# Group A's probabilities are turned in 32x32 blocks on VectorE instead of on TensorE

## The chip, the core and the metric

The kernel runs on one core of a Trainium2 chip. A core has a matrix engine (TensorE, PE in the profile, with its weight loader PEld), three engines for element-wise work (VectorE or DVE, ScalarE or ACT, GpSimd or POOL), a queue engine that mostly issues transfers (SyncE, SP), an on-chip memory of 128 partitions (SBUF) and a small accumulator memory of eight banks that TensorE writes (PSUM). The metric is the time of one execution in device microseconds. The kernel before took 2522.41 us (median of three runs, 2521.24 to 2526.48).

## What is computed

A trunk of two layers over 1024 tokens of width 1024, in float32. In each layer a normed input is projected and shared out to four groups of attention heads, whose outputs are joined, projected and added to the input; then comes an MLP with a squared ReLU.

- Group A: four heads with latent queries, keys and values; dense attention over all 1024 keys, score depth 96, value width 64.
- Group B: four differential heads; each needs two dense softmaxes, value width 64.
- Group C: banded attention over 128 tokens either side. Group D: neighbourhood attention on a 64-wide grid.

For group A the reference is, for each block of 128 queries:

```python
s = jnp.einsum('bqhd,bkhd->bhqk', qi, k, preferred_element_type=jnp.float32) * scale
p = jax.nn.softmax(s, axis=-1)
return jnp.einsum('bhqk,bkhd->bqhd', p.astype(v.dtype), v)
```

The outputs of A, C and D are each divided by their root mean square over 256 columns (the mix norm) before the output projection.

## The kernel before

Activations lie with features on partitions and tokens along the free dimension. Numbers that need float32 accuracy are split into a high and a low part, and a product takes three TensorE passes (`passes`): high x high, high x low, low x high. A split needs an activation on ScalarE and a subtraction on VectorE or GpSimd.

**Order of the work.** The program is not issued in the order in which it is written. Each engine call is recorded as a step in a plan (`Plan.add`) with a price (`Plan.price`); each stage has a window of due times (`SPAN`, in units of a layer of 1250), and a step's rank is its place in that window by TensorE's prices. `Plan.order` then imitates the engines and the transfer queues: whichever engine is free next takes, of the steps that can start, the one with the lowest rank. Steps inside `together()` are issued without a break. The resulting order is fixed in the program for each engine, so stages overlap as ranks and prices have it.

**Places.** A tile needs a place before a step can use it: 40 places of 1024 floats per partition ("pair"), 19 of 512 ("half"), some small ones, and the 8 PSUM banks. Tiles with one tag also have a cap. A place is free again when the tile's last reader is done.

**Stages of a layer** (`attention`): the projections of B, the latent inputs, D and C; `latent_up`, which makes A's queries, keys and values from the latent parts and stores them to DRAM; the attention of B, D, C and A; for each group the mix norm; the output projection in two parts. The first part, "o1", takes for four output tiles ("front") what needs groups B and D only, and for four others ("back") what needs B, D and C; each back tile then holds a PSUM bank until the second part, "o2", which needs group A's mix (mix tiles 6 and 7). Then comes the MLP, with products of 512 columns that share sums in the manner of Strassen (`mlp_up`, `mlp_down`).

**Dense attention before** (`dense`, used by A and B). For each tile of 128 queries, `softmax` makes two banks of 512 scores with three matmuls each, VectorE reduces each bank to a row minimum while it writes the negated scores to a tile p, and ScalarE takes the exponential of p with its row sum. The probabilities have queries on partitions, while the value product needs keys there. So TensorE transposes p, 128x128 at a time:

```python
nc.tensor.transpose(t[:, k * 256 + i * P:k * 256 + (i + 1) * P],
                    p[:, (j * 2 + k) * P:(j * 2 + k + 1) * P], self.ident)
```

Four transposes fill a bank, which is copied to SBUF (tag pt) by VectorE and ScalarE in turn (`transposed`). For each pair of query tiles eight float32 matmuls follow, each with 128 keys by 64 value columns as weights and 256 columns of turned probabilities moving:

```python
nc.tensor.matmul(out[k * 64:(k + 1) * 64], v[:, j * 2 + k], pts[j][:, k * 256:k * 256 + 256],
                 start=n == 0, stop=n == 3)
```

Even key tiles land in partitions 0 to 63 of the bank and odd ones in 64 to 127: two column tiles of the array. `pv_out` adds the two halves (a ScalarE copy, tag pvt, and a VectorE add into y). A float32 matmul leaves two records of TensorE in the profile. At a head's end `denominators` sends the reciprocals of the row sums through DRAM and back as a tile that is spread over partitions (rz), and y is multiplied by it.

A layer's group A so has 4 heads x 8 query tiles x 6 score matmuls, 4 x 64 transposes, 4 x 16 copies and 4 x 32 product matmuls.

**The way from group A to the second part of the projection.** y, the reciprocals' trip through DRAM, the product, squares, a column sum on TensorE (`rstd_cols`), a transpose of its result (`rows_of`), a second trip through DRAM, two products, and the split to the mix tiles (`mix_group`, `mixed`).

## Time and profile before

| | before |
|---|---|
| median of three runs | 2522.41 us |
| the profiled execution | 2517.78 us |
| its span, first to last instruction | 2516.0 us |
| mean granted TensorE clock | 0.996 |
| TensorE, weight loader | 2467.4 us, 1967.1 us |
| VectorE, ScalarE, GpSimd | 1909.8, 1290.5, 379.7 us |
| bytes moved by DMA | 378.56 MB |

The profile is that of one execution. Busy time of an engine is the union of its instructions; matmuls are pipelined, so the sum of their durations is more than their busy time. A row of a group reads: line, engine, operation, output<-inputs by the program's tile names, shapes, xcount, then busy us and mean ns of one, then the idle time of the engine in front of them and what ended it. Every instruction has the same line (677), because the plan issues them all from one place; groups are told apart by tile names: "stack" is a score operand, "p" a tile of probabilities, "ident,p" a transpose of it, "pt" turned probabilities, "bank" any PSUM tile, CUSTOM_DVE_ANT_0 the reduction to a row minimum. A row of the timeline reads: start us, duration us, engine, line, operation, tiles, shapes, xcount.

### The profile page before, as it was taken

The numbers are of one execution on the slowest core, as the hardware profiler recorded it, in microseconds if no ns is written. First come the engines' busy times: TensorE is split into PE (matmuls) and PEld (weight loads), VectorE is DVE, ScalarE is ACT, GpSimd is POOL, SyncE is SP. The second block draws the span as 40 slices with busy tenths as digits, with TensorE's granted clock in tenths as the row PEclk, the third lists the DMA queues.
The fourth block names the chain that finished last, engine by engine and source line by source line (L and its number), as shares of the span: only waits on it lengthen the run. The fifth ranks groups of instructions, "written<-read, shape, count | busy, mean of one in ns | idle before, by whom it ended". The sixth has DMA issues, their size and how long they took to land.

```text
span 2516.0 us, 35396 instructions
## 1 busy us (share of the span) xinstructions
PE 2467.4 (98%) x12332; PEld 1967.1 (78%) x12332; DVE 1909.8 (76%) x3576; ACT 1290.5 (51%) x2397; POOL 379.7 (15%) x258
## 2 busy tenths in 40 slices
PE   8999999999999999999999999999999999999998
PEld 6777776778888887888877777677788888888887
DVE  7767867775877779888777677677678777898887
ACT  4545757653644445444425456666455444444454
POOL 3323224213000000000042231332140000000000
PEclk9999999999999999999999999999999999999999
DMA  5534478622244457444154344885123444665431
GB/s 180 180 112 133 122 218 234 197 80 72 78 165 159 151 202 271 147 142 139 72 182 130 119 117 135 232 255 170 46 70 117 155 155 158 231 231 158 130 105 67
DMA packets 190514, 378.56 MB, mean 150 GB/s; under 512 B 24112, under 2 KB 36352, under 8 KB 190336
## 3 DMA queue, kind: packets, MB, share of 16 engines
q1 hardware_dynamic: 175360, 350.09, 44.6%
q10 hardware_dynamic: 14976, 26.22, 2.7%
q8 instruction: 97, 1.59, 0.3%
q14 instruction: 81, 0.66, 0.1%
HBM read 260.15 MB, written 116.07 MB: 150 GB/s over the span
## 4 chain that ended last, share of the span: by engine, by line
PE 83%; DVE 8%; DMA 4%; ACT 2%; issue 2%; SPq 1%; POOL 0%; DVEq 0%; POOLq 0%; ACTq 0%
PE bank L677 83%; DVE p L677 2%; DVE part L677 1%; SPq L677 1%; ACT p L677 1%; DVE x L677 1%; DMA a<-in_w_down 1%; DVE sq L677 1%; DMA acts<-ev 1%; DVE col L677 0%; DMA latp<-lat 0%; DMA c<-in_w_down 0%; DVE xl L677 0%; DVE ev L677 0%; DVE both L677 0%
## 5 line engine op out<-in xcount | busy, mean ns | idle before, releaser
L677 PE MATMUL bank<-far,wh 128*128 128x512 f32 (+1 forms) x2848 | 870.3, 387 | 1.1 <-ACT wh L677 0.6
L677 PEld LDWEIGHTS bank<-far,wh 128*128 128x128 f32 x2848 | 532.4, 188 | 110.5 <-ACT wh L677 1.4
L677 PE MATMUL bank<-far,wl 128*128 128x512 f32 (+1 forms) x1424 | 550.3, 387 | 2.7 <-DVE wl L677 2.7
L677 ACT ACTIVATE p<-p,col 128x1024 f32<-128x1024 f32 (+2 forms) x320 | 294.6, 921 | 196.3 <-DVE col L677 194.2
L677 POOL TENSOR_TENSOR wl<-ws,wh 128x512 fp32r<-128x512 f32 (+1 forms) x138 | 191.1, 1390 | 1180.2 <-ACT wh L677 1089.8
L677 PEld LDWEIGHTS bank<-far,wl 128*128 128x128 f32 x1424 | 267.4, 188 | 57.9 <-DVE wl L677 3.4
L677 PE MATMUL bank<-stack 96*128 96x512 f32 (+2 forms) x896 | 285.0, 395 | 5.0 <-DVE col L677 2.3
L677 DVE TENSOR_TENSOR x<-bank,x 128x512 f32<-128x512 f32 (+1 forms) x276 | 187.2, 680 | 121.9 <-PE bank L677 121.0
L677 PE MATMUL bank<-ident,p 128*128 128x128 f32 x1376 | 253.6, 276 | 10.4 <-DVE part L677 4.8
L677 PE MATMUL bank<-xh,wh 128*128 128x512 f32 x608 | 250.9, 413 | 3.1 <-ACT wh L677 2.6
L677 PE MATMUL bank<-xh,wl 128*128 128x512 f32 x608 | 250.6, 413 | 1.1 <-POOL wl L677 1.1
L677 PE MATMUL bank<-xl,wh 128*128 128x512 f32 x608 | 250.6, 412 | 0.0
L677 PEld LDWEIGHTS bank<-ident,p 128*128 128x128 f32 x1376 | 171.3, 141 | 59.5 <-issue 10.7
L677 PEld LDWEIGHTS bank<-stack 96*128 96x128 f32 (+1 forms) x896 | 159.3, 189 | 43.8 <-DVE col L677 12.1
L677 ACT ACTIVATE pt<-bank 128x512 f32<-128x512 f32 (+2 forms) x256 | 137.5, 556 | 82.9 <-PE bank L677 75.2
L677 DVE TENSOR_TENSOR wl<-raw,wh 128x512 fp32r<-128x512 f32 x224 | 150.3, 690 | 34.5 <-ACT wh L677 34.0
L677 PE MATMUL bank<-pt,v 128*64 128x256 f32 (+2 forms) x1344 | 173.1, 396 | 2.2 <-ACT pt L677 2.0
L677 ACT ACTIVATE ev<-ev 128x512 f32<-128x512 f32 x128 | 80.6, 632 | 160.3 <-DVE ev L677 155.8
L677 DVE CUSTOM_DVE_ANT_0 p<-bank,zero,col 128x512 f32<-128x512 f32 x192 | 143.8, 749 | 22.2 <-PE bank L677 5.1
L677 PE MATMUL bank<-mix,wh 128*128 128x512 f32 x512 | 160.3, 393 | 0.0
L677 DVE CUSTOM_DVE_ANT_0 p<-bank,zero 128x512 f32<-128x512 f32 x192 | 131.7, 686 | 35.4 <-PE bank L677 34.1
L677 ACT ACTIVATE wh<-raw 128x512 fp32r<-128x512 f32 x224 | 135.4, 621 | 23.8 <-ACT ev L677 10.5
(158 smaller groups left out, 3904.5 us busy)
## 6 DMA issues: line engine op xcount, KB each, us to landing
act<-acts SPq DMA_DIRECT2D x224, 256.0 KB
raw<-in_w_up SPq DMA_DIRECT2D x128, 256.0 KB
acts<-ev SPq DMA_DIRECT2D x128, 256.0 KB
acts<-ev ACTq DMA_DIRECT2D x96, 256.0 KB
ws<-in_w_in SPq DMA_DIRECT2D x76, 256.0 KB
c<-in_w_down SPq DMA_DIRECT2D x64, 256.0 KB
rz<-drows SPq DMA_DIRECT2D x40, 256.0 KB
ws<-in_w_out SPq DMA_DIRECT2D x40, 256.0 KB
```

What stands on the lines that cost most here:

```text
L677: getattr(s.eng.engine, s.op)(*[real(a) for a in s.args], **{k: real(a) for k, a in s.kw.items()})
```

## The change

For group A alone `dense` is replaced by `turned`. VectorE turns each tile of probabilities in 32x32 blocks, SBUF to SBUF: two calls of 128x512 for a query tile. A block turn leaves each block in its own strip of 32 partitions, so strip a holds, for each of the 32 key blocks of 32 keys, the queries a*32 to a*32+31 of every query tile. All eight query tiles of a head are written side by side into two new wide places of 4096 floats, so that each key block has 256 columns in each strip. The value products then are matmuls of 32 keys (one strip) by 64 value columns with 256 columns moving: 16 pairs of key blocks x 2 halves x 4 strips = 128 for a head, in one unit without a break, into four PSUM banks, one a strip. They are written for the head behind, after the third query tile's turns of the next one. The values must lie in all four strips, so `vrows` loads them four times.

The two wide places ("quad") take the room of eight pairs, so 32 pairs remain. In the other stages the wide places hold the last normed operands of the input projections, the latent parts of `latent_up`, two of `mlp_up`'s operands and the operands 1, 6, 4 and 3 of `mlp_down`. The plan's price of a float32 matmul is divided by the number of tiles that fit the array (8 for the new form) instead of by two, group A's window starts at 400 instead of 405, and o1's window is 430 to 545 instead of 505 to 550. `Plan.issue` keeps the number of tiles as its mode, and A's probabilities no longer pass through tag pt.

```diff
...
@@ -397,10 +397,10 @@
             if op == "transpose":
                 return 108.0, 53.0
             if moving.dtype == F:
-                s.tiled = cols >= 128 and (out.arr.shape[0] <= 64 or s.args[1].arr.shape[0] <= 64)
-                if s.tiled:
-                    return max(4 * cols / 2.4 + 13, 224) / 2, cols / 2.4 * 2
-                return max(4 * cols / 2.4 + 13, 224), cols / 2.4 * 4
+                tiles = 128 // max(32, out.arr.shape[0]) * (128 // max(32, s.args[1].arr.shape[0]))
+                s.tiled = tiles if cols >= 128 and tiles > 1 else 0
+                tiles = max(s.tiled, 1)
+                return max(4 * cols / 2.4 + 13, 224) / tiles, cols / 2.4 * 4 / tiles
             return (max(cols / 2.4 + 14, 112) if cols >= 128 else 112), cols / 2.4
         if q == "scalar":
             d = 0.832 * n + (50 if psum else 94)
...
@@ -598,7 +598,7 @@
             if slow:
                 occ, lat = occ * 1.89, lat * 2
             self.act[k] = self.act.get(k, 0.0) + lat
-            s.done = t + occ * (2 if s.tiled else 1) + 180 * (1.5 if slow else 1)
+            s.done = t + occ * max(s.tiled, 1) + 180 * (1.5 if slow else 1)
             return t + occ
         if q in ("vector", "gpsimd"):
             wide = [v for v in s.ins if math.prod(v.arr.shape[1:]) > 1]
@@ -625,7 +625,7 @@
         if tag in self.CAPS:
             bufs = self.CAPS[tag].get(stage, bufs)
             tag += stage
-        kind = "pair" if n > 512 else "half" if n > P else "row" if n > 16 else "col"
+        kind = "quad" if n > S else "pair" if n > 512 else "half" if n > P else "row" if n > 16 else "col"
         return self.plan.cell(shape, dt, tag="%s%d" % (tag, bufs), cap=bufs, kind=kind, name=name or tag)
 
 
@@ -651,12 +651,13 @@
         self.xp, self.big, self.wp, self.cp = place(8), place(16), place(3), place(2)
         self.place = place()
 
-    PLACES = {"pair": 40, "half": 19, "row": 3, "col": 30, "bank": 8}
+    QUADS = 2
+    PLACES = {"quad": QUADS, "pair": 40 - 4 * QUADS, "half": 19, "row": 3, "col": 30, "bank": 8}
 
     def home(self, c):
         if c.kind in self.still:
             return self.still[c.kind][c.slot]
-        n = 1024 if c.kind == "pair" else 512
+        n = {"quad": 4096, "pair": 1024, "half": 512}[c.kind]
         return self.data.tile([P, n], c.dt, tag=f"{c.kind}{c.slot}", name=f"{c.name}")
 
     def fixed(self, shape, name, dt=F):
@@ -956,8 +957,15 @@
                     self.keep(saved[k], self.x[k])
                 ahead = None
             xs, acc = [None] * 8, None
+            places = []
             for k in chain(*(range(4 * c, 4 * c + 4) for c in (l, 1 - l))):
-                h, lo = self.big_tile(R, f"xh{k}"), self.big_tile(R, f"xl{k}")
+                if not places:
+                    if k % 2 == 0 and (k % 4 // 2 + 2 * (k // 4 != l)) >= 4 - self.QUADS:
+                        q = self.place.tile([P, 4, S], R, tag="quad", bufs=self.QUADS, name="xq")
+                        places = [q[:, i] for i in range(4)]
+                    else:
+                        places = [self.big_tile(R, f"xh{k}"), self.big_tile(R, f"xl{k}")]
+                h, lo = places.pop(0), places.pop(0)
                 for sl in self.halves(1 if l or k else 2):
                     self.split(h[:, sl], lo[:, sl], self.x[k][:, sl], scale=self.g1[:, l, k:k + 1])
                 xs[k] = (h, lo)
@@ -1044,11 +1052,13 @@
                 share(self.mm_ps(), m, 1, self.weights(w_out[m, 0]) + self.weights(w_out[m, 1]), range(8))
 
     SPAN = {"open": (0, 60), "b1": (62, 95), "lat": (270, 325), "pd": (95, 170), "pc": (170, 270), "b": (65, 330),
-            "d": (230, 390), "up": (335, 390), "c": (300, 405), "a": (405, 510), "mb": (345, 350), "md": (405, 410),
-            "mc": (415, 420), "ma": (515, 520), "o1": (505, 550), "o2": (550, 600), "mlp": (600, 1220)}
+            "d": (230, 390), "up": (335, 390), "c": (300, 405), "a": (400, 510), "mb": (345, 350), "md": (405, 410),
+            "mc": (415, 420), "ma": (515, 520), "o1": (430, 545), "o2": (550, 600), "mlp": (600, 1220)}
     LAYER, SOON, IDLE = 1250, 20, 12
-    BANKS = {"mm": 8, "tr": 4, "sb": 2, "pv": 2}
+    BANKS = {"mm": 8, "tr": 4, "sb": 2, "pv": 2, "pq": 4}
     EARLY, NP = 4, 6
+    AFTER = 2
+    WIDE = {6, 4, 3}
     WAVES = [(T_BQ[t], T_BK[t], T_BV[t]) for t in range(2)]
 
     def table(self, name, rb, eng):
@@ -1186,14 +1196,16 @@
 
     def latent_up(self, l, lat, rows, qa, ka, va):
         nc, d = self.nc, self.d
-        rq, rkv = self.big_tile(F, "rq"), self.big_tile(F, "rkv")
+        quads = [self.place.tile([P, 4, S], R, tag="quad", bufs=self.QUADS, name="latp") for _ in range(2)]
+        rq, rkv = (quads[1][:, i].bitcast(F) for i in (2, 3))
+        tiles = iter([quads[0][:, i] for i in range(4)] + [quads[1][:, i] for i in range(2)])
         self.spread(rq, rows[0], 0, 2)
         self.spread(rkv, rows[0], 1, 2)
         parts = []
         for i, r in ((0, P), (1, 64), (2, P)):
             p = []
             for j in range(2):
-                t = self.big_tile(R, "latp")
+                t = next(tiles)
                 for at in range(0, P, r):
                     self.load(t.bitcast(F)[at:at + r], lat[j, i, :r])
                 p.append(t)
@@ -1358,6 +1370,59 @@
             products()
         yield True
 
+    def vrows(self, src):
+
+        src = src.rearrange("(q r) k d -> r q (k d)", q=4)
+        tiles = []
+        for i in range(2):
+            v = self.place.tile([P, 2, 8, 64], F, tag="vr", bufs=4, name="v")
+            for a in range(4):
+                self.load(v[a * 32:a * 32 + 32].rearrange("p q k d -> p q (k d)"), src[:, 2 * i:2 * i + 2])
+            tiles.append(v)
+        return tiles
+
+    def turned(self, heads):
+
+
+        nc = self.nc
+        rows = [slice(a * 32, a * 32 + 32) for a in range(4)]
+
+        def products(job):
+            t, v, y, h2, done = job
+            pv = [self.bank("pq")[:, 0:256] for _ in rows]
+            with self.plan.together():
+                for n in range(16):
+                    for c in range(2):
+                        k, q = divmod(2 * n + c, 4)
+                        for r, ps in zip(rows, pv):
+                            nc.tensor.matmul(ps[c * 64:c * 64 + 64], v[q // 2][r, q % 2, k], t[n // 8][r, 2 * n + c & 15],
+                                             start=n == 0, stop=n == 15)
+            o = y[h2 * 64:h2 * 64 + 64].rearrange("p (t a j) -> p a t j", a=4, j=32)
+            for i in range(2):
+                other = self.place.tile([P, 512], F, tag="pt", bufs=self.NT, name="pvt")[0:64]
+                for j in range(2):
+                    ps, e = pv[2 * i + j], other[:, j * 256:j * 256 + 256]
+                    nc.scalar.activation(e, ps[64:128], AF.Copy)
+                    self.tt(o[:, 2 * i + j], ps[0:64].rearrange("p (t j) -> p t j", j=32),
+                            e.rearrange("p (t j) -> p t j", j=32), ALU.add)
+            done()
+
+        job = None
+        for head in heads:
+            probs, *rest = head()
+            t = [self.place.tile([P, 16, 256], F, tag="quad", bufs=self.QUADS, name="turn") for _ in range(2)]
+            for i in range(8):
+                p = probs(i)
+                for n in range(2):
+                    nc.vector.transpose(t[n][:, :, i * 32:i * 32 + 32],
+                                        p[:, n * 512:n * 512 + 512].rearrange("p (b j) -> p b j", j=32))
+                if i == self.AFTER and job:
+                    products(job)
+            job = (t, *rest)
+            yield True
+        products(job)
+        yield True
+
     def attn_b(self, l, t, qb, kb, vb, out):
         nc = self.nc
         pair = {}
@@ -1430,7 +1495,7 @@
                 tl.append(s[0:96])
             qh, kh, ql, kl = tl
             passes = [(qh, kh), (qh, kl), (ql, kh)]
-            v = self.vtile(va[h])
+            v = self.vrows(va[h])
             z = self.col("za", 8)
 
             def probs(qt):
@@ -1443,7 +1508,7 @@
 
             return probs, v, y, h2, done
 
-        yield from self.dense([lambda h=h: head(h) for h in range(4)])
+        yield from self.turned([lambda h=h: head(h) for h in range(4)])
         ys += [y for y, _ in out]
 
 
@@ -1637,6 +1702,10 @@
         t = self.place.tile([P, 2, 512], dt, tag=tag, bufs=bufs, name=tag)
         return t[:, 0], t[:, 1]
 
+    def wide(self):
+        t = self.place.tile([P, 4, 2, 512], R, tag="quad", bufs=self.QUADS, name="wide")
+        return [(t[:, k, 0], t[:, k, 1]) for k in range(4)]
+
     def rows_split(self, t, src, scale=None):
 
         self.split(t[0], t[1], src, scale)
...
@@ -1791,7 +1860,7 @@
                 for s in first:
                     s.w11 = self.weight_parts(s.c["11"], "we", 4)
                     combos(s.c)
-            places = [near(c) for c in "abc"]
+            places = [near() if i < self.QUADS else [self.twin("opc", R) for _ in range(4)] for i in range(3)]
             ops[2] = [self.rows_split(places[0][k], x(k + 4, 0), gk(k + 4)) for k in range(4)]
             for s in first:
                 p12(s)
@@ -1874,14 +1943,15 @@
                     return out
 
                 def op(o):
-                    return [self.rows_split(self.far(), t) for t in raw_op(o)]
+                    to = self.wide() if o in self.WIDE else [self.far() for _ in range(4)]
+                    return [self.rows_split(p, t) for p, t in zip(to, raw_op(o))]
 
                 M = range(4)
                 u = [self.bank("u") for _ in M]
                 with self.plan.sooner(0 if j else self.SOON):
                     a11 = [w(2 * i + e, 0, t) for i in range(2) for e, t in enumerate(self.twin("a"))]
                     t = raw_op(1)
-                b = [self.rows_split(self.far(), v) for v in t]
+                b = [self.rows_split(p, v) for p, v in zip(self.wide(), t)]
                 for m in M:
                     self.block(u[m], a11[m], b)
                     add(m, 0, u[m])
```

More of the change, by code (lines that the diff above doesn't have):

```diff
@@ L316, in add @@
         s.unit.steps.append(s)
-        s.start, s.tiled = None, False
+        s.start, s.tiled = None, 0
         before = set()
@@ L452, in order @@
         self.act, self.slow, self.window = {}, {0: True}, 0
-        self.mode = False
+        self.mode = 0
         for u in units:
@@ L1674, in mlp_up @@
         with self.banks(u=2, p=2, q=2, mm=2):
-            near = lambda tag: [self.twin("op" + tag, R) for _ in range(4)]
+            near = self.wide
             far = self.far
```

## The prediction

> **What bounds the kernel now.** I read the page's head first, then its chain, then busy time by stretch, then the stretch in which group A is computed, by groups of instructions.
>
> ```profile
> span 2516.0 us, 35396 instructions
> ...
> PE 2467.4 (98%) x12332; PEld 1967.1 (78%) x12332; DVE 1909.8 (76%) x3576; ACT 1290.5 (51%) x2397; POOL 379.7 (15%) x258
> ...
> PE 83%; DVE 8%; DMA 4%; ACT 2%; issue 2%; SPq 1%; POOL 0%; DVEq 0%; POOLq 0%; ACTq 0%
> ```
>
> TensorE is busy for 98% of the span and makes 83% of the chain that ended last: what is taken off TensorE shortens the time, as long as nothing else becomes the bound. That has to be read by stage. In layer 0, 442 to 549 is group A's attention (its first score matmul starts at 442.01), 549 to 600 mostly the first half of the output projection, 600 to 645 its second half; 1684 to 1791 is group A again in layer 1.
>
> ```profile
> core 0: us, PE busy (x) PEld busy (x) DVE busy (x) ACT busy (x) POOL busy (x), PEclk, DMA share, GB/s
> 340.00:442.00 102.00, 95.67 (x577) 70.38 (x577) 70.90 (x187) 68.00 (x176) 42.09 (x28) 0.98 0.85 243
> 442.00:549.00 107.00, 106.55 (x715) 80.56 (x714) 80.19 (x192) 72.95 (x126) 19.85 (x10) 1.00 0.50 151
> 549.00:600.00 51.00, 51.00 (x255) 40.91 (x254) 25.70 (x39) 14.61 (x29) 11.80 (x11) 1.00 0.18 50
> 600.00:645.00 45.00, 45.00 (x201) 37.24 (x200) 38.26 (x49) 29.37 (x51) 21.26 (x14) 1.00 0.27 74
> ...
> 1684.00:1791.00 107.00, 106.07 (x709) 79.74 (x707) 79.80 (x190) 72.10 (x125) 19.79 (x10) 1.00 0.51 150
> ```
>
> In group A's stretch TensorE has no hole (106.55 of 107), but VectorE stands at 80.19 already. The two layers agree, so I work out layer 0 and double it. A full 512-column matmul costs TensorE 0.224 us (201 in 45.00). The groups of the stretch 442 to 549, and rows of TensorE and of its weight loader in order of time:
>
> ```profile
> L677 PE MATMUL bank<-stack 96*128 96x512 f32 x192 | 54.1, 411 | 0.0
> L677 PE MATMUL bank<-ident,p 128*128 128x128 f32 x248 | 35.8, 275 | 0.1
> ...
> L677 PE MATMUL bank<-pt,v 128*64 128x256 f32 x228 | 27.9, 386 | 0.0
> L677 DVE CUSTOM_DVE_ANT_0 p<-bank,zero,col 128x512 f32<-128x512 f32 x32 | 24.0, 749 | 4.1 <-PE bank L677 0.6 <-DVE col L677 0.2
> L677 DVE CUSTOM_DVE_ANT_0 p<-bank,zero 128x512 f32<-128x512 f32 x32 | 22.0, 686 | 6.4 <-PE bank L677 6.3
> L677 DVE COPY pt<-bank 128x512 f32<-128x512 f32 x29 | 19.9, 686 | 10.8 <-PE bank L677 10.8
> L677 ACT ACTIVATE pt<-bank 128x512 f32<-128x512 f32 x30 | 17.6, 587 | 10.8 <-PE bank L677 10.7
> ...
> L677 DVE TENSOR_TENSOR y<-bank,pvt 64x512 f32<-64x512 f32 x7 | 4.8, 680 | 0.1
> ```
> ```profile
> 442.01 0.48 PE L677 MATMUL bank<-stack 96*128 96x512 f32 x1
> ...
> 505.01 1.95 PE L677 MATMUL bank<-pt,v 128*64 128x256 f32 x16
> ...
> 508.16 1.04 PE L677 MATMUL bank<-ident,p 128*128 128x128 f32 x8
> ```
> ```profile
> 507.93 1.03 PEld L677 LDWEIGHTS bank<-ident,p 128*128 128x128 f32 x8
> ```
>
> The reader is to see three prices. A transpose takes (1.04 - 0.275)/7 = 0.109 us from start to start. A product matmul leaves two records, and two column tiles run abreast: 16 records are 8 rounds, (1.95 - 0.386)/7 = 0.22 us a round. And VectorE's half-score copy, its negated-score reductions and its adds over 512 columns all take about 0.69.
>
> **The change part by part.** Per layer group A has 4 heads of 8 query tiles.
>
> Removed from TensorE: 4 x 64 transposes x 0.109 = 27.9 us. Removed with them: 64 copies out of PSUM, 32 on VectorE (32 x 0.686 = 22.0) and 32 on ScalarE (18.8, off the path).
>
> Added to VectorE: 16 block turns a head, 64 a layer, of 128x512. No row shows one. Bounds: 0.553 and 1.299, a copy of 384 columns and an operation that passes over 1024:
>
> ```profile
> L677 DVE COPY pt<-bank 128x384 f32<-128x384 f32 x48 | 26.5, 553 | 17.1 <-PE bank L677 16.6
> L677 DVE TENSOR_TENSOR sq<-sq 128x1024 f32<-128x1024 f32 x20 | 26.0, 1299 | 2.3 <-ACT sq L677 2.3
> L677 DVE TENSOR_TENSOR part<-bank,rb 128x256 f32<-128x256 f32 x48 | 18.1, 419 | 24.6 <-PE bank L677 24.5
> ```
>
> I take 0.686, the copy of the same shape: 43.9 a layer. The result adds become 16 of 256 columns (0.419, 6.7) instead of 8 of 512 (5.4). VectorE in the stretch: 80.2 - 22.0 + 43.9 + 1.3 = 103.4 of 107.
>
> Products: 128 matmuls of 32 rows by 64 columns a head, 256 records, instead of 64. If all eight tiles run abreast these are 32 rounds x 0.22 = 7.0 us, as now (32 rounds). No row shows row tiles side by side. Bounds: 7.0, and 256 x 0.11 = 28.2 if only the column pair overlaps. I take 7.0, because the pair shows that tiles are independent. One entry into the tiled mode a head goes instead of two; the drain is a fraction of a microsecond, nothing.
>
> The Trainium skill speaks against the full factor ("TensorE: Matmul & The Clock Gate", Part 3: Packing small matmuls): four row tiles were measured at 3.07 times, not 4. By it a head's products would take 9.1 us, by my row 7.0; the sum below would end 17 us later, at an estimated 2512, inside the forecast's own range. No run here shows it yet.
>
> So TensorE's own work for group A falls to about 107 - 28 = 79 us and VectorE's rises to 103: **VectorE becomes the bound of this stage.** The output projection's first part is moved forward (its window now starts at 430) to fill TensorE. It can't fill all: the products take four PSUM banks, the scores two, and each of the four back tiles holds a bank to the second half.
>
> A new wait: the two wide places hold one head. The next head's turns wait until the products have read them, the first place after half (3.5 us), the second after 7.0. Queued behind that on VectorE is the next head's softmax: one tile's pair of reductions is ready (0.749 + 0.686 = 1.4), then VectorE is out of scores, since TensorE is in the products. It idles about 2 us in the first half and 1.6 after three turns (3 x 0.69) in the second: 3.6 a head, 11 over three changes. VectorE's other work here (scaling, mixing; 9.5 us, what the four groups above leave of 80.2) covers some of it. I take 8.
>
> End of group A: 442 + 103.4 + 8 = 553.4, then the last head's products 7.0 and their reading 1.5: 562 (now 559.0, below). Then comes the chain of norms that nothing shortens but less waiting:
>
> ```profile
> 558.34 0.69 DVE L677 TENSOR_TENSOR y<-bank,pvt 64x512 f32<-64x512 f32 x1
> ...
> 569.12 1.23 DVE L677 TENSOR_TENSOR sq<-sq 128x1024 f32<-128x1024 f32 x1 [1.13 <-ACT sq L677]
> ...
> 575.22 1.84 PE L677 MATMUL bank<-ones,sq 128*128 128x1 f32 x16
> ...
> 578.08 0.17 DVE L677 SCALAR_TENSOR_TENSOR col<-col,col 128x8 f32<-128x8 f32 x1
> ...
> 583.18 0.27 PE L677 MATMUL bank<-ident,col 128*8 128x128 f32 x1
> ...
> 592.42 2.55 ACT L677 ACTIVATE mix<-y,par 128x512 fp32r<-128x512 f32 x4
> ...
> 644.07 0.39 PE L677 MATMUL bank<-mix,wl 128*128 128x512 f32 x1
> ```
>
> It lasts 592.4 - 559.0 = 33.4, of which 575.22 - 570.35 = 4.9 and 583.18 - 578.25 = 4.9 are waits for a TensorE that was busy with the projection. TensorE has holes now, so 9.2 of these go: 24.2. Group A's mix stands at 586.2, its first half is split 1.4 later (0.64 on ScalarE, by the row of four, 0.69 on VectorE, and the hand-over), and 192 matmuls x 0.224 = 43.0 are left: 630.6, against 644.3 now. Gain 13.7 a layer, **27.4 in all**. If TensorE's holes also take the 24 matmuls of the front tiles that need only group C, 5.4 more a layer.
>
> At nothing, with cover: values are fetched four times over, in 8 transfers of 128 KB a head instead of one of 256 KB, into a stretch where DMA is at 0.50; SP's extra issues are short, there are places for two heads' values, and these are needed only 20 us after a head's first score. The latent parts and the MLP's operands move into the wide places: same instructions, same operand depth, TensorE full there. Forty paired places become 32 beside the wide ones: bound, from nothing to the 6.3 us in which TensorE already waits in 340 to 442 (95.67 of 102) doubled; I take nothing.
>
> The profiled execution took 2517.78 us (1.8 around its span), 4.6 below the median of 2522.41, a gap of its own runs' spread. I subtract from the median: 2522.4 - 27.4 = **2495**. No change that can be measured means within 0.2% (5 us).
>
> **The rivals.**
>
> *TensorE stays the bound.* The whole 27.9 a layer comes off: 2522.4 - 55.8 = 2467. For it: packed, VectorE starts operations of 0.67 only 0.60 apart, so that the sum of 103.4 could pass in about 93 with other work behind it.
>
> ```profile
> 561.84 0.67 DVE L677 TENSOR_TENSOR wl<-raw,wh 128x512 fp32r<-128x512 f32 x1
> 562.44 0.67 DVE L677 TENSOR_TENSOR raw<-raw 128x512 f32<-128x512 f32 x1
> 563.04 0.67 DVE L677 TENSOR_TENSOR x<-bank,x 128x512 f32<-128x512 f32 x1
> ```
>
> Against it: the wait for the wide places, and the chain of 24 after the last head.
>
> *The gain is given back in front.* With 8 places fewer for groups B, C, D and the latent stage, group A's first score slides from 442 to 456: 2522, no change. For it: TensorE already idles in that stretch with DMA at 0.85. Against: the 16 normed operands that fill these places earlier use the wide ones too.
>
> *Product tiles are bound by their weights: slower.* Eight transposes start 0.109 apart, although 128 columns stream in 0.056; what takes 0.109 is the load of 128 columns, so 64 take 0.055. If 256 loads a head go one after another, products take 14.1, 7.1 more, on the path that VectorE waits on: 4 x 7.1 = 28.4 - 13.7 = 14.7 a layer later, 2552. It decides from 7.0 + 13.7/4 = 10.4 us a head, 41 ns a record. With row tiles fully in turn, 28.2 a head, it is 2522 + 2 x (84.8 - 13.7) = 2665. For it: nothing in the trace issues so densely; 16 loads and 16 matmuls in 1.95 us is the most, and this asks for four times that.
> By the skill's same part, loads overlap running matmuls where the row group differs; then the 14.1 falls away. No row here shows it.
>
> *A turn costs VectorE two passes: slower.* At 1.299, 64 x 0.613 = 39.2 more a layer: 2522 + 2 x (39.2 - 13.7) = 2573. It decides from 0.90 us a turn.
>
> **How the numbers follow.** Forecast 0.42, own range 2484 (24 matmuls taken early in both layers) to 2515 (products at 9 instead of 7 us a head, 8 more a layer, or no wait covered, 3 us a layer from the fewer places, and a lower granted clock in TensorE's holes, as the 0.98 of 340 to 442). TensorE stays the bound 0.16. Given back in front 0.12, of which 0.03 faster, 0.07 within 0.2%, 0.02 slower. Weight-bound or serial tiles 0.20, of which 0.07 near 2665. Slow turns 0.10. Faster 0.61, same 0.07, slower 0.32. Range 2460 to 2556: it takes in all but the serial tiles and the slow turns, 17 in 100.
>
> **What would show it.** Right: turns of about 0.69, VectorE above 95% and TensorE near 85% in group A's stretch, a head's products within 7 to 9 us, no transposes of p there, mix matmuls beginning well before the last scores, the second half of the projection about 14 us earlier in each layer, the MLP's rows unchanged. Wrong: products over 10.4 us a head, turns over 0.90, or the first score after 450.

## The result, and the profile after

The kernel after takes 2531.2 us (median of five runs, 2521.5 to 2534.6), the kernel before on the same chip 2521.5 (five runs, 2521.2 to 2526.5): ratio 1.0038, 95% interval 1.0027 to 1.0050. The change is **slower by 0.4%**; I had forecast 2495, 1.1% faster. 2531 lies inside the range of 2460 to 2556, on the side to which I had given 0.32.

The head of the page of the kernel after, TensorE's clock by slices, and the chain:

```profile
span 2528.8 us, 37471 instructions
...
PE 2434.8 (96%) x13356; PEld 1944.2 (77%) x13356; DVE 1946.5 (77%) x3656; ACT 1257.0 (50%) x2349; POOL 378.3 (15%) x258
...
PEclk9999999898999999999999999998989999999999
...
PE 80%; DVE 11%; DMA 4%; issue 3%; ACT 2%; SPq 1%; POOL 0%; DVEq 0%; POOLq 0%; ACTq 0%
```

TensorE is busy for 32.6 us less than before (2434.8 against 2467.4), yet the span is 12.8 longer. The slices at 8 in the clock's row are new; in each layer one stands where group A begins and one where it ends. Busy time by stretch, from the end of the opening's matmuls to the end of the output projection, layer 0 and layer 1, first before, then after:

```profile
core 0: us, PE busy (x) PEld busy (x) DVE busy (x) ACT busy (x) POOL busy (x), PEclk, DMA share, GB/s
360.40:644.50 284.10, 277.31 (x1634) 211.55 (x1633) 201.93 (x429) 172.58 (x353) 92.42 (x61) 0.99 0.50 148
1604.30:1886.90 282.60, 276.63 (x1634) 210.87 (x1633) 200.01 (x428) 172.31 (x353) 92.25 (x61) 1.00 0.50 149
```
```profile
360.00:654.90 294.90, 264.10 (x2144) 201.41 (x2143) 220.42 (x468) 153.96 (x327) 91.74 (x61) 0.91 0.52 153
1614.50:1900.60 286.10, 257.55 (x2145) 197.78 (x2144) 217.44 (x468) 153.89 (x327) 91.62 (x61) 0.93 0.54 157
```

Every such stretch can be split in three: TensorE's **work** (busy time, with the time in stretches of clock 0.50 counted half), its **idle** time, and what the **half clock** cost (the other half of that busy time). Sums over both layers, in us, from the profiled execution of each kernel of this study (busy and length are those of the rows above; the half-clock part is TensorE's busy time inside the pieces of the clock's record at 0.50, halved):

| kernel | stretch | work | idle | half clock | median us |
|---|---|---|---|---|---|
| before | 566.7 | 552.2 | 12.8 | 1.7 | 2521 |
| after | 581.0 | 491.0 | 59.4 | 30.6 | 2531.2 |
| e9, windows earlier | 562.0 | 493.2 | 40.7 | 28.1 | 2513.9 |
| e12, windows of the change alone | 598.7 | 555.1 | 33.2 | 10.4 | 2554.1 |

So the 61 us of TensorE's work that the change takes off (30.6 a layer) are gone as planned, and 46.6 us of idle time and 28.9 us of half clock have come in their place. The rest of the program is as long as before within 1.5 us. Where the idle time lies: TensorE's waits in layer 0, from the latent stage's end to the projection's end, first before, then after.

```profile
engine line waited for: us in total, times, longest us
PE bank L677 <- DVE sq L677: 0.4, 1, 0.4
```
```profile
PE bank L678 <- DVE sq L678: 9.7, 2, 9.2
PE bank L678 <- ACT mix L678: 8.7, 2, 7.2
PE bank L678 <- DVE col L678: 2.6, 3, 1.2
PE bank L678 <- DVE turn L678: 2.3, 1, 2.3
```

Two holes make most of it. The **front hole** is in head 0 of group A. TensorE's instructions, then ScalarE's and VectorE's, in order of time (start, length, and in brackets the idle time before and what ended it):

```profile
445.79 9.79 PE L678 MATMUL bank<-stack 96*128 96x512 f32 x42
456.48 1.66 PE L678 MATMUL bank<-stack 96*128 96x512 f32 x6 [0.89 <-DVE col L678]
467.31 1.87 PE L678 MATMUL bank<-ones,sq 128*128 128x1 f32 x8 [9.18 <-DVE sq L678]
```
```profile
463.22 1.15 ACT L678 ACTIVATE p<-p,col 128x1024 f32<-128x1024 f32 x1 [0.34 <-DVE col L678]
...
464.37 1.04 ACT L678 ACTIVATE sq<-y 128x1024 f32<-128x1024 f32 x1
```
```profile
464.85 1.30 DVE L678 STREAM_TRANSPOSE turn<-p 128x512 f32<-128x512 f32 x2
466.07 1.18 DVE L678 TENSOR_TENSOR sq<-sq 128x1024 f32<-128x1024 f32 x1
```

TensorE runs the scores of head 0 and nine matmuls of head 1 nearly without a stop, ahead into free banks, and then stands at the column sums of group D's norm. These need a sum of squares: the last square is in ScalarE's queue behind head 0's exponentials, which wait for VectorE's reductions, and its add is in VectorE's queue behind the last turns of head 0. VectorE's rows follow each other from 452 on, with pauses of at most 0.15 us. Whatever else TensorE could do is behind the column sums in its own queue. The **tail hole** is at the other end, after the last head:

```profile
596.73 1.84 PE L678 MATMUL bank<-ones,sq 128*128 128x1 f32 x16
599.81 0.38 PE L678 MATMUL bank<-ident,col 128*8 128x128 f32 x1 [1.24 <-DVE col L678]
607.42 1.22 PE L678 MATMUL bank<-mix,wh 128*128 128x512 f32 x2 [7.24 <-ACT mix L678]
```

The norm's row goes to DRAM and back, is multiplied in and mixed; no matmul of the projection's first part is left to cover it. Behind both holes the clock is at half:

```profile
438.70:459.70 21.00, 18.54 (x97) 13.40 (x95) 17.97 (x45) 13.10 (x23) 9.33 (x7) 1.00 0.95 259
459.70:480.20 20.50, 12.89 (x129) 10.00 (x137) 11.52 (x31) 8.67 (x15) 2.36 (x1) 0.50 0.29 88
480.20:599.60 119.40, 111.63 (x1284) 87.50 (x1268) 90.17 (x195) 46.86 (x91) 22.75 (x16) 0.94 0.43 125
599.60:613.30 13.70, 6.25 (x15) 4.62 (x16) 6.71 (x10) 3.90 (x7) 0.00 (x0) 0.50 0.11 39
613.30:654.90 41.60, 41.40 (x183) 33.93 (x182) 38.18 (x47) 26.64 (x46) 19.70 (x13) 1.00 0.22 71
```

The second and fourth rows are the stretches of half clock; four shorter ones of 3.4 us each lie in the third row. And the new instructions themselves, by groups (438 to 655), and a head's products at full clock:

```profile
L678 DVE STREAM_TRANSPOSE turn<-p 128x512 f32<-128x512 f32 x64 | 41.8, 687 | 19.1 <-PE bank L678 17.8 <-ACT p L678 1.4
...
L678 PE MATMUL bank<-turn,v 32*64 32x256 f32 x1024 | 35.5, 434 | 4.1 <-DVE turn L678 2.3 <-issue 1.8
```
```profile
548.36 7.16 PE L678 MATMUL bank<-turn,v 32*64 32x256 f32 x256
```

A turn takes 0.687 us and a head's products 7.16: the prices of the prediction hold, and the loss is not in them.

### The profile page after: what moved, and what is told of

It reads as the page before. It is cut to its first block, busy times and chain, and to the rows that moved or that the text cites. A ratio compares the mean times of both kernels' runs of the same rounds, so it can differ in the third digit from the quotient of the medians.

```text
span 2528.8 us, 37471 instructions
## 1 busy us (share of the span) xinstructions
PE 2434.8 (96%) x13356; PEld 1944.2 (77%) x13356; DVE 1946.5 (77%) x3656; ACT 1257.0 (50%) x2349; POOL 378.3 (15%) x258
## 4 chain that ended last, share of the span: by engine, by line
PE 80%; DVE 11%; DMA 4%; issue 3%; ACT 2%; SPq 1%; POOL 0%; DVEq 0%; POOLq 0%; ACTq 0%
PE bank L678 80%; DVE p L678 3%; DVE part L678 2%; DVE turn L678 1%; DVE x L678 1%; ACT p L678 1%; DVE col L678 1%; SPq L678 1%; DMA x<-in_x 0%; DMA rz<-drows 0%; DMA c<-in_w_down 0%; DVE acc L678 0%; DVE sq L678 0%; DVE ev L678 0%; DVE both L678 0%
## 5 line engine op out<-in xcount | busy, mean ns | idle before, releaser
L678 PE MATMUL bank<-far,wh 128*128 128x512 f32 x1792 | 552.9, 389 | 0.5 <-ACT ev L678 0.5
L678 PE MATMUL bank<-wide,wh 128*128 128x512 f32 (+1 forms) x1568 | 475.0, 385 | 0.0
L678 PEld LDWEIGHTS bank<-far,wh 128*128 128x128 f32 x1792 | 336.0, 188 | 70.8 <-ACT ev L678 1.3
L678 PE MATMUL bank<-far,wl 128*128 128x512 f32 x896 | 348.6, 389 | 0.0
L678 PEld LDWEIGHTS bank<-wide,wh 128*128 128x128 f32 x1568 | 292.4, 188 | 58.7
L678 PE MATMUL bank<-wide,wl 128*128 128x512 f32 (+1 forms) x784 | 301.6, 385 | 2.2 <-DVE wl L678 2.2
L678 PE MATMUL bank<-xq,wh 128*128 128x512 f32 x608 | 211.3, 411 | 0.0
L678 PEld LDWEIGHTS bank<-far,wl 128*128 128x128 f32 x896 | 168.2, 188 | 34.9
L678 PE MATMUL bank<-ident,p 128*128 128x128 f32 x864 | 178.1, 277 | 10.5 <-DVE part L678 4.4
L678 PEld LDWEIGHTS bank<-wide,wl 128*128 128x128 f32 x784 | 147.3, 188 | 32.3 <-DVE wl L678 3.0
```

Of the source, the lines that this page charges most:

```text
L678: getattr(s.eng.engine, s.op)(*[real(a) for a in s.args], **{k: real(a) for k, a in s.kw.items()})
```

## The experiments

Theory: TensorE has too little other work beside VectorE's turns and in the last chain of norms; it idles, and its clock goes to half. Rivals: the fewer paired places; the wide places that hold one head only; the projection moved forward; VectorE's sum. Each group of runs stands beside runs of the kernel before on the same chip (medians 2520.9 to 2521.9); the interval is that of the ratio to it. Only e5 and e6 keep the planned order of the kernel after; in the other runs the order changes with the edit.

**e1: the places alone.** The kernel after with the windows of before and

```
-        yield from self.turned([lambda h=h: head(h) for h in range(4)])
+        yield from self.dense([lambda h=h: head(h) for h in range(4)])
```


> The wide places are there and hold what the change gives them in the opening, the latent stage and the MLP, but group A's heads are computed as before (transposes, copies, products) and the windows are those of before. If the fewer paired places cost time (the rival that the gain is given back in front): 10 us a layer more, about 2540. If TensorE running dry inside group A is the cause: no difference from before that can be told, 2522 within 5 us.

2522.4 us, ratio 1.0007 (0.9998 to 1.0017). The places cost nothing that can be told (at most 0.17%); that rival falls.

**e2: the windows of before.**

```
-            "a": (400, 510), "o1": (430, 545)
+            "a": (405, 510), "o1": (505, 550)
```


> The turns and the products in tiles as in the change, but group A and the first part of the output projection keep the windows of before (405 to 510, 505 to 550). If the projection moved forward uncovers the last chain of norms, the hole of 8.5 us there and the half clock behind it (6 us of matmuls at half speed, 3 us) go, 11.5 a layer: about 2508. If TensorE lacks work in group A wherever the projection stands, the holes only move to where VectorE sets the pace: 2531 or above, to 2545.

2547.1, ratio 1.0108 (1.0091 to 1.0125). The second expectation, even over its end. The tail's wait shrinks to 2.5 us in layer 0, but inside group A there are now holes of 7.0, 3.3, 5.2 and 5.7. The forward move is worth 16 us to the turned form.

**e3: a third wide place.**

```
-    QUADS = 2
+    QUADS = 3
```


> Three wide places instead of two (28 paired places left), so that a head's first turns need not wait until the products of the head before have read theirs. If the single-buffered places are the cause: VectorE's waits of turns for TensorE (17.8 us in layer 0) go, of which at least half shows, 2 x 9: about 2513. If TensorE's two long holes and the half clock behind them are the cause, these stay and the time too: 2531 within 5 us.

2580.0, ratio 1.0237 (1.0221 to 1.0252): far outside both. VectorE's waits in layer 0 after the latent stage:

```profile
DVE p L678 <- PE bank L678: 16.7, 11, 9.6
...
DVE turn L678 <- PE bank L678: 4.0, 1, 4.0
```

The turns' wait for TensorE fell from 17.8 to 4.0 us, and no time was won: VectorE now waits for scores instead (16.7 against 5.7). But the third place also takes four paired places, and loads for the scores come late (TensorE waits 4.9 and 2.3 us for them), so this run cannot say what a third place alone would be worth. That stays open; a third wide place beside all the paired ones was not tried.

**e4 to e6: TensorE kept busy in the holes.** Matmuls of zeros into a bank that nothing reads, in TensorE's queue at the place where it waits; the planner counts them as nothing.

```
+    def fill(self, ps, n):
+        for _ in range(n):
+            self.nc.tensor.matmul(ps, self.zero, self.zero[:, 0:1].broadcast_to([P, 512]), start=True, stop=True)
+            self.plan.steps[-1].cost = 0.0, 0.0
```


> Only change against the kernel after: 40 matmuls of zeros (about 9 us) stand in TensorE's queue ahead of the column sums of group D's norm and 32 (about 7 us) ahead of the first matmul of the projection's second part, where TensorE waits 9.2 and 7.2 us anyway; the planner counts them as nothing, so that the order stays. If the half clock that follows the two holes costs the time: TensorE runs the 12.9 and 5.9 us behind them at full clock, 9.4 us a layer less, about 2512. If only the waits cost, and the half clock lies beside VectorE's pace: no less than 2526. If the filling itself delays what stands behind it: above 2531.

2537.4, ratio 1.0075 (1.0057 to 1.0092). The third expectation, for a reason that the trace shows: the 32 zeros for the tail stood behind the first eight matmuls of the second part, so the hole of 7.2 stayed and the zeros came on top. The front filling did what was meant, so the two were parted.

> Only the 40 matmuls of zeros ahead of the column sums of group D's norm, where TensorE waits 9.2 us in the kernel after. In the run with both fillings layer 0 came from the end of the latent stage (438.2 or 441.5) to the last product in 134.0 us against 145.8, layer 1 in 136.2 against 138.8. If the half clock behind this hole costs the time: 11.8 and 2.6 us come back, about 2517. If this was VectorE's pace in disguise: 2528 to 2531.

2521.8 (ten runs), ratio 1.0001 (0.9990 to 1.0011): 9.4 us less than the kernel after, most of the first expectation. Apart from the zeros, each engine's instructions have the order of the kernel after. TensorE's rows:

```profile
460.61 9.01 PE L678 MATMUL bank<-zero 128*128 128x512 f32 x40
469.92 1.05 PE L678 MATMUL bank<-ones,sq 128*128 128x1 f32 x8 [0.30 <-DVE sq L678]
470.84 1.64 PE L678 MATMUL bank<-stack 96*128 96x512 f32 x6
```

The column sums come as late as before, since VectorE sets that; but eight of them take 1.05 us instead of 1.87 and six scores 1.64 instead of 2.91, and so does what follows. This is the half clock priced by itself: work that is useless, in a hole that stays as long, makes the kernel 0.4% faster. (The profiled execution is the slowest of its ten, 2528.7; in it layer 0 gains 11.9 us from the latent stage's end to the projection's end, and layer 1 loses 4.2 to other stretches of half clock.)

> Only 32 matmuls of zeros (about 7 us), now directly behind the last norm's transpose in TensorE's queue: in the run with both fillings they stood behind the first matmuls of the second part and so behind the hole. If the half clock behind the hole costs the time: the 5.9 us of matmuls that ran at half clock after it are 3 us shorter a layer, about 2525. If the wait alone counts (the chain through the two transfers of the norm's row): 2531 within 2 us. If the filling outlasts the hole: above 2533.

2531.4, ratio 1.0036 (1.0022 to 1.0049): nothing won. The zeros outlasted the hole:

```profile
594.86 0.27 PE L678 MATMUL bank<-ident,col 128*8 128x128 f32 x1 [1.24 <-DVE col L678]
594.89 8.91 PE L678 MATMUL bank<-zero 128*128 128x512 f32 x32
603.63 1.09 PE L678 MATMUL bank<-mix,wh 128*128 128x512 f32 x4
```

From the transpose to the first mix matmul it is 8.8 us instead of 7.6. From the last product to the projection's end it is 68.8 instead of 70.5 in both layers, 1.7 better a layer, too little for these runs to tell.

**e7 and e8: the first heads as before.**

```
-        yield from self.turned([lambda h=h: head(h) for h in range(4)])
+        yield from self.dense([lambda: head(0, self.vtile)])
+        yield from self.turned([lambda h=h: head(h, self.vrows) for h in range(1, 4)])
```


> Head 0 of group A is computed as before (64 transposes on TensorE, copies, products), heads 1 to 3 as in the change. If TensorE lacks work while VectorE turns head 0 alone (the projection has nothing ready yet): the 7 us of transposes fill the hole of 9.2, VectorE loses 16 turns, no half clock there; of the 20.9 us taken off TensorE the tail's hole and its half clock (8.5 and 3) and 5 us of small holes go: 4 a layer better than before, about 2514. If every head is held back alike by VectorE and the two wide places: about 2529.

> Heads 0 and 1 as before, 2 and 3 as in the change: 14 us a layer off TensorE. If holes come only from head 0 and the tail: 14 - 11.5 = 2.5 a layer better than before, about 2517. If every turned head costs what it gives (as after does over four): half of after's loss, about 2526.

2528.6, ratio 1.0026 (1.0015 to 1.0037), and 2534.1, ratio 1.0053 (1.0038 to 1.0068). The first is at its second expectation, the second slower than both of its own. The front hole is gone in both, and the half clock falls from 30.6 to 17.8 and 14.9. But the work rises by 16.9 and 30.7, and the tail's 8.5 us and waits of 2.5 to 4.2 before products, whose last turns come late, remain. Giving TensorE its transposes back fills holes with work that was just taken off.

**e9, e10, e14: the windows earlier and later.**

```
-            "a": (400, 510), "o1": (430, 545)
+            "a": (380, 495), "o1": (430, 575)
```


> The kernel after with two windows changed: group A from 380 to 495 (not 400 to 510), the projection's first part from 430 to 575 (not to 545), so that head 0 is scored and turned beside the matmuls of groups D and C and more of the projection is left for the last chain. If TensorE's lack of other work beside VectorE's turns is the cause: the front hole (9.2) and the half clock behind it (6.4) go and a part of the tail's 8.5, say 5: 20 us a layer, 2491. If the turned form itself holds group A back (VectorE's sum, the two wide places): 2525 or above.

2513.9, ratio 0.9965 (0.9952 to 0.9978): **faster than both kernels**, 0.35% than before, though 23 us short of what I expected. TensorE's waits in layer 0:

```profile
PE bank L678 <- issue: 5.6, 3, 3.8
PE bank L678 <- ACT mix L678: 3.4, 1, 3.4
PE bank L678 <- DVE col L678: 2.4, 3, 1.2
PE bank L678 <- DVE sq L678: 2.4, 1, 2.4
```

The waits of 9.2 and 7.2 are down to 2.4 and 3.4. The idle time of the table falls by 19 us, but the half clock only by 2.5: several holes of 2 to 4 us have taken the place of two long ones, and each can cost stretches of 3.4 us and more.

> Only group A's window is earlier (380 to 500), the projection's as in the kernel after. If the front hole is the larger part: it and its half clock go, 2 x 15.6, and the tail stays: 2500. If the projection's end matters as much, the work that it took from the tail leaves a longer hole there: 2515 to 2520. If neither matters: 2531.

> The kernel after with only the projection's first part ending later (430 to 575), group A at 400 to 510. If the cover of the last chain alone made e9 faster: 8.5 us of hole and 3 of half clock go, 2 x 9: 2513. If it takes both (work beside head 0 and work left for the tail): 2525 to 2535.

2531.2, ratio 1.0035 (1.0022 to 1.0048), and 2535.1, ratio 1.0050 (1.0031 to 1.0069). One of the two windows alone wins nothing: with group A earlier (to 500, not 495) and the projection ending as in the change, the tail's wait is 7.15 us again; with the projection's end alone moved, the front hole is 9.17. The idle time is 59.0 and 59.5 us and the half clock 29.1 and 30.9, against 59.4 and 30.6 in the kernel after: what one hole gives back, others take. It takes both windows.

**e11: half of every turn.**

```
-                    nc.vector.transpose(t[n][:, :, i * 32:i * 32 + 32],
-                                        p[:, n * 512:n * 512 + 512].rearrange("p (b j) -> p b j", j=32))
+                    nc.vector.transpose(t[n][:, 0:8, i * 32:i * 32 + 32],
+                                        p[:, n * 512:n * 512 + 256].rearrange("p (b j) -> p b j", j=32))
```


> Each turn takes 256 of its 512 columns and the products read the turned half twice: half of the probabilities is left out, the matmuls are the same in number and size. VectorE has 64 x 0.3 = 19 us a layer less. If it is VectorE's turning that lets TensorE run dry: the front hole shrinks from 9.2 to under 4, group A ends about 8 us earlier, 2531 - 2 x 8 = 2515 or less. If the amount on VectorE doesn't count, only the order and the clock: 2531 within 5.

2519.2, ratio 0.9995 (0.9986 to 1.0005), 12 us less than the kernel after: between the two. The wait before the column sums is gone, and 3.05 and 3.75 us stand before head 0's products in its place. That fits the turns as the maker of the front hole, but the shorter turns also changed the planned order (head 0's products now stand ahead of the column sums), so this run doesn't show the amount alone. A turn of 256 columns takes 0.420 us instead of 0.687, 34 us less on VectorE over the two layers, and only 12 return. In the profiled execution, the fastest of its ten, the idle time falls by only 5 (54.0) and the half clock by 12 (18.9): a new hole of 5.6 and 5.1 opens later in the group, where TensorE waits for a transfer of score operands, and the tail's 7.2 stays.

**e12: the windows of the change in the kernel before.**

> The kernel before with the two windows of the change (group A from 400, the projection's first part 430 to 545) and nothing else. If moving the projection forward takes the cover from the last chain, also without turns: a hole of about 8 us before the second part, with half clock behind it, 10 a layer, 2542. If the cover is lost only because the turned heads end late: 2522 within 5.

2554.1, ratio 1.0130 (1.0115 to 1.0145): the first expectation, and 12 us more. The tail's wait is there without a single turn (layer 0):

```profile
PE bank L677 <- ACT mix L677: 7.2, 1, 7.2
```

The moved projection uncovers the last chain by itself. That is 33 us of loss in the old form; in the change the turned form gives back 23 of it. With e2 this makes a square: neither part 2521, the windows alone 2554, the turned form alone 2547, both 2531. Each part alone loses more than the two together.

**e13, e15, e16: what e9 rests on.** The kernel before with group A's window at 380 to 495; e9 with the zeros of e6; e9 with the half turns of e11.

> The kernel before with group A's window at 380 to 495 and nothing else. TensorE was busy there for 201.9 of 202.4 us, so no order can give it more: 2521 or slower, to 2530, if what e9 gained comes from filling TensorE beside VectorE's turns. If the early start is worth something by itself, e9's gain belongs to the window: 2511 to 2515.

> e9 with 32 matmuls of zeros behind the last norm's transpose. There the hole is 3.4 and 2.5 us only (7.2 in the kernel after), so that 7 us of filling outlast it by about 4 a layer; the half clock behind it (3.4 us stretches, 1.5 us) goes. If the chip's time follows TensorE's queue: 2 x 2.5 slower than e9, 2519. If the half clock weighs more than it seems: 2510 or less.

> e9 with half of each turn left out, the products reading the turned half twice (half of the probabilities is missing). VectorE has 19 us a layer less. If TensorE is kept from work by VectorE's turns also in this order (17 and 14 us idle, 13 and 9 lost to the half clock after the latent stage): about half of it returns, 13 a layer, 2488. If the rest is order and clock, not VectorE's amount: 2508 or above.

e13: 2528.4, ratio 1.0027 (1.0016 to 1.0038). The early start slows the old form, so e9's gain doesn't belong to group A's window alone. The old form with both windows of e9 was not run, so how much of e9's gain is the turns' is not shown. e15: 2521.0, ratio 1.0001 (0.9990 to 1.0012), 7 slower than e9: zeros that outlast a hole are plain cost. e16: 2507.9, ratio 0.9935 (0.9912 to 0.9958), 6 less than e9 (the two intervals still overlap) for some 34 us of VectorE's time: the amount on VectorE is not the main limit in this order either.

## Why the prediction was wrong

- **Removed from TensorE, right.** 27.9 us of transposes a layer; the work fell by 30.6.
- **A turn at 0.686, right:** 0.687. VectorE's busy time over the stretch rose by 18.5 and 17.4 us a layer (201.9 to 220.4 and 200.0 to 217.4); I had 23.2. Slow turns fall.
- **Products at 7.0 us a head, right:** 7.16 at full clock, (7.16 - 0.43)/255 = 26.4 ns from record to record, eight tiles in 0.211 us where a pair took 0.22. The rival of weight-bound or serial tiles falls (it decided from 41 ns). By the Trainium skill, "TensorE: Matmul & The Clock Gate", Part 3, four row tiles gain 3.07 times (there with 512 moving columns), which made 9.1 us by my estimate. This trace does not agree, it shows the full factor. (I counted two entries into the tiled mode a head before; the trace shows four. The term stood at nothing.)
- **The places and the latent stage at nothing, right** (e1). Given back in front: falls; the first score of group A came at 441.3, not at 456.
- **The chain of norms: a little shorter than forecast, its half clock left out.** From the last adds to group A's mix it takes 20.3 us (586.4 to 606.65), where I had 24.2. Of the projection's first part 12.4 us of matmuls were left in the 23.0 from the last product to the first matmul of the second part; the norm's own matmuls took 2.2, and TensorE idled for the other 8.4 and went on at half clock.
- **The step that failed: "VectorE becomes the bound of this stage", and with it "End of group A: 442 + 103.4 + 8".** I set the length of the stage equal to the sum of the busier engine, with one wait added. In the terms of that sum this is the whole miss of layer 0: the last adds ended at 586.4, not at 562, the chain was 3.9 shorter, the second part took 47.5 us and not 43.0, and the projection ended at 654.9, not at 630.6. The last product ended at 584.4, with VectorE busy for 107.3 of these 142.4 us, 75% and not 95:

```profile
442.00:584.40 142.40, 125.59 (x1407) 96.33 (x1404) 107.27 (x245) 60.94 (x110) 28.03 (x18) 0.88 0.49 141
```

 Neither engine bounds it. In head 0 VectorE is full and TensorE empty (the front hole); in heads 1 to 3 TensorE is nearly full (111.6 of 119.4 us), because the projection's matmuls now stand between the scores, and VectorE waits for it (turns 17.8 us, where I had 8; scores 5.7). An engine's sum bounds a stage only if the other's queue always has something ahead to do, and here both are in order.
- **The projection moved forward was costed at nothing.** I named it as filling for TensorE, as if its matmuls took nothing from group A and had covered nothing where they stood. My sum did hold the whole chain of norms with nothing under it, so the uncovered chain is not what put the sum off; its price in the sum is the half clock behind it, in the 47.5 us above. But the gain in time that the sum gave rested on group A ending at 562 although the projection now runs inside it. e12 gives the price of the two windows in the old form, 33 us; e2 shows that with the windows of before the turned form is 16 us worse still.
- **The lower clock was in the wrong place.** I had it as a small part of my own range's upper end, by the 0.98 of another stretch. In this stretch it was 0.91 and 0.93 and cost 28.9 us over both layers. I had counted idle time of TensorE, an engine that was no longer to be the bound, as free; e5 shows that the clock charges for it later.

Of the rivals none happened; the loss was the forecast's own mechanism with its two costs left out. What the runs leave open is the share of the wide places (e3), and what the old form would take with both windows of e9. Why e9 keeps 28 us of half clock is answered in part in the last section.

## What to carry to other kernels

When work is taken off an engine that was full, ask what will stand in its queue in each part of the stage, and which chain the moved work had been covering; the gain is only what the queue can fill. On TensorE a hole can cost twice: its own length, and half of the matmuls' time behind it until the clock is back; filling it with useless work pays only while the filling ends before the wait does (e5 against e6 and e15). Move windows together and measure them: here each alone won nothing, and both gave the only version with all of the work that is faster than either kernel.

## What the hardware showed

The half clock comes in pieces of 3.4 us: 3.4, 6.8, 10.2, 13.7, 17.1 and 20.5 in these traces; in each of the 18 traces they all begin on one grid of 3.413 us, within 0.005 us. The Trainium skill, "TensorE: Matmul & The Clock Gate", Part 1, gives a free-running window of 3413 ns, half clock after an idle one and full after a busy one. The length and the grid agree; the rule agrees only in part. The table counts the windows of this grid between 300 and 2490 us in all 18 traces (a count of TensorE's records against the clock's), by the share of the window that TensorE was busy and by the number of records of matmuls that stream a single column (the column sums):

| clock | TensorE busy | column sums | windows | half clock in the next |
|---|---|---|---|---|
| full | under 50% | none | 84 | 73 |
| full | 50 to 88% | none | 444 | 24 |
| full | 96% or more | none | 9883 | 1 |
| full | 96% or more | 14 or more | 78 | 15 |
| half | 96% or more | none | 136 | 4 |
| half | 96% or more | one or more | 44 | 39 |

A wholly idle window isn't needed: one that is more than half idle is enough as a rule. And a busy window brings the clock back, but seldom one with column sums in it. So it went behind the front hole: TensorE's records show it busy from 467.3 on, and the clock was back only at 480.2. Of the three whole windows in between, the first two hold column sums, the last has none. In e9 a hole of 2.4 us before column sums was followed by 13.7 us of half clock in the same way. By the records TensorE was busy, for the clock it seems not to have been; no run moved the column sums alone, so that they are the cause is likely, not shown.

The times of the kernel after scatter over 13 us. In e5 the faster executions had the higher mean clock (2516.5 us at 0.989, 2528.7 at 0.984), but the fastest and the slowest of the kernel after both had 0.980; what scatters them is not shown.

Matmuls of 32 rows by 64 columns started 26.4 ns apart over a whole head, eight tiles side by side. I had not expected so dense an issue, with 256 weight loads among them, to hold.
